# Attention stage: row loads ahead of the weights, five raw tiles for the input weights, query absorption between the token rows

## The chip, the cores and the metric

One core of a Trainium2 chip. The time is that of one execution of the whole program on the device, in microseconds (us); lower is better. The kernel before took 3136.23 us in the median of three runs (3130.83, 3138.18, 3136.23).

## What is computed

Two decoder layers over 1024 tokens of width 1024, in fp32. Layer 0: RWKV-7 time mixing, then a gated feed-forward network (FFN). Layer 1: sparse attention (DSA), then an FFN. Each part ends in a residual and a layer norm. The change lies at the start of the attention, which computes

```python
h = x @ w_in                                   # 1024 x 456: c_q 256 | c_kv 128 | k_idx 64 | w_idx 8
c_q, c_kv = rms_norm(c_q, ...), rms_norm(c_kv, ...); k_idx = layer_norm(k_idx, ...)
q = c_q @ w_uq                                 # 16 heads of 64
q_abs = einsum('bthd,hdc->bthc', q, w_uk)      # logits = q_abs . c_kv * 64**-0.5
```

The kernel forms the product of `w_uq` and `w_uk` once ("absorbs" them; the scale 0.125 is 64**-0.5), so that `q_abs` needs one product per token. Each fp32 matrix product is made of three matmuls on a high and a low part (`mm3`); `split` makes the parts: a cast to the high part on ScalarE, a subtraction for the low part on GpSimd or VectorE.

## The kernel before, in words

The four parts (`rwkv`, `ffn`, `dsa`, `ffn`) are generators, which `drive` interleaves: the start of one is written amid the end of the one before. All instructions are handed to a planner, which fixes each engine's order when the kernel is built: of the instructions whose inputs its own time model holds ready, it takes the one that stands earliest in the program. On the chip every engine, and SP's queue of DMA issues, runs its list strictly in that order.

The end of the first FFN is the product with `w_down` (tile `dn`, lines 65 to 67 by way of `d_mm`). For the second half of the tokens, pairs p = 0 to 8 run over all eight outputs; `d_end` then adds the last two pairs output by output and evicts at L1173: first the four column halves `ch` = 1, after which the attention's first lines are written (L1275 to L1307), then the four halves `ch` = 0 (12 matmuls each). After each of these four, `d_norm` normalizes one 128-row group (L98 to L111 on VectorE, ScalarE and GpSimd) and SP stores it (L149). These are token groups 4 to 7; groups 0 to 3 were stored over 100 us earlier.

The attention's start, in program order: load `uq` and `uk`; the absorption (L1278 to L1295: 64 matmuls into eight banks `wqk`; per bank a scaled copy on ScalarE to `o`, a cast to `hi` on ScalarE, `lo` on GpSimd, two stores to `wqk` in DRAM); eight `w_in` tiles, each loaded into a raw tile `wr` (tag `qr`, two tiles) and split into `win`; the row `grow`. Then come eight steps: `x_load(tt)` loads one token group in two halves (tag `u`, six tiles), and from the third step on `early(2)` takes two entries of a list: `x_T` (eight transposes `pt` and a split into X) and `w_in` (24 matmuls `win` and the norms). Steps 0 to 3 are written before the four last `d_end`, steps 4 to 7 one behind each. After that the hidden rows are transposed (`h_T`, L1368), and the index queries, the indexer, top-k and attention follow.

Where tiles lie matters. Tiles of a pool lie behind one another in the order in which their tags are first used. The attention's pool begins 11 KB (per partition) below the space of the first FFN's pool, and a tile can only be written when the FFN tiles at its addresses are done with. The FFN's pool holds twelve tiles of 4 KB at 11 to 59 KB (tokens `hr`, `hh`, `hl`) and three weight tiles of 16 KB at 59 to 107 KB, which go round by pair. Before, the attention has `u` at 0 to 12 KB, `ph` 12 to 18, `win` 18 to 50, `qr` 50 to 54, `kv` to 58, and three tiles `big` (X and others) to 106.

Of the kernel before, what the change touches and what calls it, by code (L numbers as in the profile page):

```python
# [8 lines left out]
F32R = mybir.dt.float32r  # L9
BF16 = mybir.dt.bfloat16  # L10
AF = mybir.ActivationFunctionType
ALU = mybir.AluOpType
# [33 lines left out]
def f32(ap):  # L46
    return ap.bitcast(F32)


def split(k, raw, hi, lo, hi_eng="a", lo_eng="p"):  # L50

    nc = k.nc
    if hi_eng == "a":
        nc.scalar.copy(hi, raw)  # L54
    elif hi_eng == "v":
        nc.vector.tensor_copy(hi, raw)
    else:
        nc.gpsimd.tensor_scalar(hi, raw, 1.0, 0.0, ALU.mult, ALU.add)
    eng = nc.vector if lo_eng == "v" else nc.gpsimd
    eng.tensor_tensor(lo, raw, f32(hi), ALU.subtract)  # L60
# [1170 lines left out]
def dsa(k, src, dst):  # L1231
    nc, tc = k.nc, k.tc
# [6 lines left out]
    def u(name, dt=F32):  # L1239
        return P_.tile([128, 512], dt, name=name, tag="u", bufs=6)  # L1240

    def tagged(pool, tag, bufs, cols=512):
        return lambda name, dt=F32: pool().tile([128, cols], dt, name=name, tag=tag, bufs=bufs)

    p_, m_ = lambda: P_, lambda: M_
    qr, ph_, qw = tagged(p_, "qr", 2), tagged(p_, "ph", 3), tagged(m_, "qw", 4)
    cm_, ol_ = tagged(m_, "cm", 3, 256), tagged(m_, "ols", 1)

    def w4(name, shape=(128, 1024), dt=F32):
        return P_.tile(list(shape), dt, name=name, tag="tmp", bufs=8)  # L1250

    def ps_tile(tag, name):
        bufs = {"l": 4, "tp": 2, "o": 1, "ol": 1}[tag]
        return (PL if tag == "l" else PS).tile([128, 512], F32, name=name, tag=tag, bufs=bufs)

    def acc(name):
        return ps_tile("l", name)

    def big(name, shape):
        return P_.tile(list(shape), F32R, name=name, tag="big", bufs=3)  # L1260
# [6 lines left out]
    def x_load(tt):  # L1267
        rows[tt] = []
        for g in range(2):
            xr = u("xr")  # L1270
            nc.sync.dma_start(xr, src[tt * 128 : tt * 128 + 128, 512 * g : 512 * g + 512])
            rows[tt].append(xr)


    wqk = k.dram.tile([8, 2, 128, 512], F32, name="wqk")  # L1275
    uq = T_.tile([128, 8, 256], F32, name="uq", tag="toep", bufs=1)
    nc.sync.dma_start(uq, k.w_uq.rearrange("p (h c) -> p h c", h=8))
    for h4 in range(2):  # L1278
        uk = u("uk")
        nc.sync.dma_start(uk, k.w_uk[:, 512 * h4 : 512 * h4 + 512])  # L1280
        for g in range(2):
            gs = slice(64 * g, 64 * g + 64)
            for kt in range(2):
                ps = acc("wqk")
                for h in range(4):
                    hc = slice(128 * h, 128 * h + 128)
                    nc.tensor.matmul(
                        ps[:, hc], uq[gs, 4 * h4 + h, 128 * kt : 128 * kt + 128], uk[gs, hc], start=True, stop=True
                    )
                o, lo = u("wqk"), u("wqkl", F32R)  # L1290
                nc.scalar.activation(o, ps, AF.Copy, scale=0.125)
                hi = ph_("wqkh", F32R)
                split(k, o, hi, lo, "a", CFG["quq"])
                for j, w in enumerate((hi, lo)):
                    nc.sync.dma_start(wqk[4 * g + 2 * h4 + kt, j], f32(w))  # L1295
    win = []
    for kt in range(KT):
        wt = w4("win", (128, 2, 512), F32R)
        raw = qr("wr")
        nc.sync.dma_start(raw[:, :456], k.w_in[kt * 128 : (kt + 1) * 128, :])  # L1300
        split(k, raw[:, :456], wt[:, 0, :456], wt[:, 1, :456], "a", "pv"[kt % 2])
        win.append(wt)
    grow = ph_("grow")
    nc.sync.dma_start(grow, k.dsa_rows[0:1, :].to_broadcast([128, 512]))
    kv = P_.tile([128, 8, 128], F32, name="kv")
    widx = P_.tile([128, 8, 8], F32, name="widx")
    yield  # L1307
# [67 lines left out]
    LAG = CFG['lag']  # L1375
# [7 lines left out]
    def early(n):  # L1383
        for _ in range(n):
            f, tt = pend.pop(0)
            r = f(tt)
            if f is w_in:
                done[0] = r

    for tt in range(8):  # L1390
        x_load(tt)
        if tt >= LAG:
            early(2)
        yield
    M_, PS = pools.add("dsm", first=True, side="left"), pools.psum("dsps", side="left")
    XTh = M_.tile([128, 4, 1024], F32R, name="XTh")
# [18 lines left out]
    for kt in range(2):  # L1415
        raw = qr("wr")
# [481 lines left out]
def trunk(tc, *args):  # L1898
    with ExitStack() as es:
        k = setup(tc, args[:-1], es)  # L1900
        out = args[-1]
        x1, x2, x3 = (Rows(k.dram, f"x{i}") for i in (1, 2, 3))
        drive([rwkv(k, k.x, x1), ffn(k, 0, x1, x2), dsa(k, x2, x3), ffn(k, 1, x3, out)])
# [33 lines left out]
```

## Time and profile before

| | |
|---|---|
| median of three runs | 3136.23 us (3130.83 to 3138.18) |
| profiled execution, its time | 3131.68 us |
| its span, first to last instruction | 3129.9 us |
| TensorE (PE) busy | 2852.7 us, 91% |
| VectorE (DVE), GpSimd (POOL), ScalarE (ACT) busy | 69%, 45%, 43% |
| mean granted TensorE clock | 0.944 of full speed |

The profile is that of one execution. All times below are counted from its first instruction. A line such as L65 is a line of the kernel; helpers such as `mm3` and `split` keep one line for all callers, and the tile names tell them apart. "Idle before" is the time in which the engine stood still just before a group, with what ended it.

### The profile page before, as it was taken

Reading aid. Unit: us, or ns where it says so; the run is one execution under the profiler, and the core shown is the slowest. Engines: PE = TensorE matmul, PEld = TensorE weight load, DVE = VectorE, ACT = ScalarE, POOL = GpSimd, SP = SyncE. Lnnn points to the kernel's source line nnn. Section 1 sums busy time; section 2 is a strip of 40 time slices with the busy share of each in tenths; the row PEclk is TensorE's granted clock in tenths of the full one; section 3 lists DMA queues with packets and bytes.
Section 4 is the critical chain, followed back from the end, with each engine's and each line's share of the span. In section 5 each row is a group of like instructions: output and inputs, shape, how many; then the busy total and the mean of one; then the engine's idle time right before and its main releaser. Section 6 shows DMA issues by size and latency. Waiting matters only on the chain. (4 is left out here: it accounts for less than half of the span.)

```text
span 3129.9 us, 41844 instructions
## 1 busy us (share of the span) xinstructions
PE 2852.7 (91%) x15260; PEld 2249.3 (72%) x15260; DVE 2161.4 (69%) x3609; ACT 1358.0 (43%) x2340; POOL 1406.9 (45%) x947
## 2 busy tenths in 40 slices
PE   7789798899888899999997888889898899999997
PEld 3577666787766777778886766656786677777886
DVE  6777767857676788886142599996575888887142
ACT  4534134232233444444342487785363544444430
POOL 3515115131155677765474122112213667666762
PEclk9889889989899999999999889899999999999999
DMA  6645435435235222235544221113215133333740
GB/s 212 242 146 193 133 106 190 160 106 197 86 120 184 61 81 78 76 90 199 177 168 140 89 86 48 38 34 112 84 46 166 52 81 81 81 94 116 281 168 27
DMA packets 247808, 377.96 MB, mean 121 GB/s; under 512 B 18506, under 2 KB 112074, under 8 KB 247218
## 3 DMA queue, kind: packets, MB, share of 16 engines
q1 hardware_dynamic: 233778, 350.12, 34.3%
q10 hardware_dynamic: 13824, 25.17, 2.2%
q8 instruction: 120, 1.97, 0.3%
q14 instruction: 86, 0.70, 0.1%
HBM read 272.06 MB, written 103.15 MB: 120 GB/s over the span
## 5 line engine op out<-in xcount | busy, mean ns | idle before, releaser
L60 POOL TENSOR_TENSOR wo<-wr,wo 128x512 fp32r<-128x512 f32 x220 | 408.9, 1882 | 290.1 <-ACT wo L54 283.1
L1045 DVE SCALAR_TENSOR_TENSOR cv<-u,vec,cv 128x1023 f32<-128x1023 f32 (+1 forms) x176 | 343.0, 1966 | 58.0 <-ACT cv L1040 56.3
L60 POOL TENSOR_TENSOR wd<-dr,wd 128x1024 fp32r<-128x1024 f32 x88 | 224.8, 2582 | 134.9 <-ACT wd L54 134.9
L67 PE MATMUL dn<-wd,hl 128*128 128x512 f32 x704 | 274.0, 389 | 0.0
L65 PE MATMUL dn<-wd,hh 128*128 128x512 f32 x640 | 249.0, 389 | 0.0
L66 PE MATMUL dn<-wd,hh 128*128 128x512 f32 x640 | 249.0, 389 | 0.0
L65 PE MATMUL p<-xT,wo 128*128 128x512 f32 x528 | 213.3, 404 | 25.7 <-ACT u L1029 19.3
L67 PE MATMUL p<-xT,wo 128*128 128x512 f32 x528 | 208.6, 395 | 5.9 <-POOL wo L60 5.9
L1040 ACT ACTIVATE cv<-u,vec 128x1024 f32<-128x1024 f32 x88 | 109.5, 1245 | 240.2 <-DVE u L1034 240.1
L66 PE MATMUL p<-xT,wo 128*128 128x512 f32 x528 | 208.9, 396 | 3.0 <-DVE xT L60 3.0
L1632 POOL TENSOR_TENSOR cm<-sc,toep 128x256 f32<-128x256 f32 x96 | 75.3, 790 | 296.1 <-DVE mn L1648 227.8
L60 POOL TENSOR_TENSOR wo<-S,wo 128x512 fp32r<-128x512 f32 x88 | 176.3, 2022 | 29.5 <-ACT wo L54 29.5
L60 DVE TENSOR_TENSOR hl<-hr,hh 128x1024 fp32r<-128x1024 f32 x36 | 57.6, 1601 | 160.5 <-ACT hh L54 100.0
L60 POOL TENSOR_TENSOR wl<-wr,wh 128x512 fp32r<-128x512 f32 x56 | 77.6, 1385 | 185.5 <-ACT wh L54 148.7
L67 PEld LDWEIGHTS dn<-wd,hl 128*128 128x128 f32 x704 | 132.2, 188 | 27.5
L65 PEld LDWEIGHTS p<-xT,wo 128*128 128x128 f32 x528 | 100.5, 190 | 63.9 <-ACT u L1029 34.5
L65 PE MATMUL p<-x,wo 128*128 128x512 f32 x352 | 138.5, 394 | 2.9 <-DVE x L60 2.5
L54 ACT CAST wd<-dr 128x1024 fp32r<-128x1024 f32 x88 | 89.3, 1050 | 115.2 <-DMA dr<-in_w_down_dram 51.1
L54 ACT CAST wo<-wr 128x512 fp32r<-128x512 f32 x220 | 126.9, 617 | 26.5 <-POOL wo L60 17.8
L65 PEld LDWEIGHTS dn<-wd,hh 128*128 128x128 f32 x640 | 120.1, 188 | 25.1
L66 PE MATMUL p<-x,wo 128*128 128x512 f32 x352 | 137.9, 392 | 0.0
L66 PEld LDWEIGHTS dn<-wd,hh 128*128 128x128 f32 x640 | 120.1, 188 | 24.7
(403 smaller groups left out, 8130.2 us busy)
## 6 DMA issues: line engine op xcount, KB each, us to landing
wr<-in_w_up_dram SPq DMA_DIRECT2D x88, 512.0 KB, 5.9
dr<-in_w_down_dram SPq DMA_DIRECT2D x88, 512.0 KB, 3.7
hd<-cv SPq DMA_DIRECT2D x44, 512.0 KB, 3.4
hr<-hd SPq DMA_DIRECT2D x44, 512.0 KB, 4.5
wr<-in_w_wo_dram SPq DMA_DIRECT2D x68, 256.0 KB, 3.0
wr<-in_w_rkv_dram SPq DMA_DIRECT2D x48, 256.0 KB, 4.2
kept_w<-wh ACTq DMA_DIRECT2D x48, 256.0 KB, 3.1
kept_w<-wl SPq DMA_DIRECT2D x48, 256.0 KB, 3.1
```

The source lines that it names most:

```text
L54: nc.scalar.copy(hi, raw)
L60: eng.tensor_tensor(lo, raw, f32(hi), ALU.subtract)
L65: mm(ps, lhs[0], rhs[0], start=start, stop=False, **kw)
L66: mm(ps, lhs[0], rhs[1], start=False, stop=False, **kw)
L67: mm(ps, lhs[1], rhs[0], start=False, stop=stop, **kw)
L1040: nc.scalar.activation(o, u, AF.Identity, bias=k.vec[:, cb : cb + 1], scale=k.vec[:, cw[2] : cw[2] + 1])
L1045: nc.vector.scalar_tensor_tensor(o[:, d:], u[:, : 1024 - d], k.vec[:, cw[j] : cw[j] + 1], o[:, d:], ALU.mult, ALU.add)
L1632: (nc.vector if CFG["cm"][h4] == "v" else nc.gpsimd).tensor_tensor(cm[:, :near], mk, toep[g][:, h % 8, 256 - near :], ALU.add)
```

## The change

The loads of token groups 0 and 1 come first. The raw tiles for `w_in` come from two tags, `qr` (two tiles) and `ph` (three). `uq` and `uk` are loaded behind `w_in` and `grow`, `uk` in one DMA into a `big` tile; since `big` is now the first tag used, the pool is laid out as `big` 0 to 48 KB, `u` to 60, `win` to 92, `qr` to 96, `ph` to 102, `kv` to 106. The absorption moves to step 4, thus behind the first of the last four `d_end`. It no longer makes the copy `o`: ScalarE writes `hi` from PSUM with the scale, and VectorE makes `lo` from PSUM; both are `u` tiles. The list of `x_T` and `w_in` is taken at another pace, so that six of its entries instead of four are written ahead of the first of the last four `d_end`.

```diff
+    uk = big("uk", (128, 8, 512))
+
+    def absorb_load():
+        nc.sync.dma_start(uq, k.w_uq.rearrange("p (h c) -> p h c", h=8))
+        nc.sync.dma_start(f32(uk[:, :2]), k.w_uk.rearrange("p (h c) -> p h c", h=2))
+
+    def absorb():            # the same loops and matmuls as before, in a function
...
-                o, lo = u("wqk"), u("wqkl", F32R)
-                nc.scalar.activation(o, ps, AF.Copy, scale=0.125)
-                hi = ph_("wqkh", F32R)
-                split(k, o, hi, lo, "a", CFG["quq"])
+                    hi, lo = u("wqkh", F32R), u("wqkl", F32R)
+                    nc.scalar.activation(hi, ps, AF.Copy, scale=0.125)
+                    nc.vector.scalar_tensor_tensor(lo, ps, 0.125, f32(hi), ALU.mult, ALU.subtract)
...
+    for tt in range(2):
+        x_load(tt)
     win = []
     for kt in range(KT):
         wt = w4("win", (128, 2, 512), F32R)
-        raw = qr("wr")
+        raw = (ph_ if kt % 5 > 1 else qr)("wr")
...
     nc.sync.dma_start(grow, k.dsa_rows[0:1, :].to_broadcast([128, 512]))
+    absorb_load()
...
     for tt in range(8):
-        x_load(tt)
-        if tt >= LAG:
-            early(2)
+        if tt == 4:
+            absorb()
+        if tt >= 2:
+            x_load(tt)
+        early((0, 0, 2, 4, 1, 2, 2, 2)[tt])
         yield
```

## Rows read from the trace of the kernel before

**Rows 1.** Windows of 20 us: busy time and count by engine, clock, DMA.

```profile
1680.00:1700.00 20.00, 18.98 (x117) 16.10 (x116) 10.17 (x27) 12.09 (x24) 12.03 (x11) 1.00 0.53 180
1700.00:1720.00 20.00, 2.70 (x13) 2.15 (x13) 6.40 (x13) 7.95 (x18) 13.16 (x12) 0.66 0.65 230
1720.00:1740.00 20.00, 20.00 (x104) 18.27 (x103) 10.61 (x34) 6.33 (x19) 6.56 (x9) 0.91 0.85 280
```

**Rows 2.** PE's timeline: start, length, operation, count, idle before.

```profile
1682.60 0.39 PE L65 MATMUL dn<-wd,hl 128*128 128x512 f32 x1
1682.92 3.50 PE L1287 MATMUL wqk<-uk,uq 64*128 64x128 f32 x32
...
1695.38 3.47 PE L1287 MATMUL wqk<-uk,uq 64*128 64x128 f32 x32 [1.02 <-DMA uk<-in_w_uk_dram]
...
1700.96 0.39 PE L67 MATMUL dn<-wd,hl 128*128 128x512 f32 x1
1718.64 3.65 PE L1318 MATMUL pt<-ident,xr 128*128 128x128 f32 x16 [17.30 <-DMA xr<-x]
1721.94 0.73 PE L65 MATMUL win<-win,X 128*128 128x456 f32 x1
...
1727.78 1.03 PE L1318 MATMUL pt<-ident,xr 128*128 128x128 f32 x8
1728.58 0.45 PE L65 MATMUL win<-win,X 128*128 128x456 f32 x1
...
1733.64 1.03 PE L1318 MATMUL pt<-ident,xr 128*128 128x128 f32 x8
...
1757.96 0.60 PE L1368 MATMUL ht<-ident,hn 128*128 128x128 f32 x4
```

**Rows 3.** SP's queue of DMA issues, timeline.

```profile
1660.13 24.81 SPq L1300 DMA_DIRECT2D wr<-in_w_in_dram  x8
...
1712.67 0.39 SPq L1304 DMA_DIRECT2D grow<-in_dsa_rows_dram  x1
1713.11 9.52 SPq L1271 DMA_DIRECT2D xr<-x  x10
```

**Rows 4.** What SP's queue waited for, 1640 to 1760 us: total, times, longest.

```profile
SPq L1295 <- POOL wqkl L60: 10.0, 8, 2.8
```

**Rows 5.** ScalarE's and VectorE's timelines: first cast and last split of `win`.

```profile
1671.02 1.05 ACT L54 CAST win<-wr 128x456 fp32r<-128x456 f32 x2 [30.36 <-PE dn L66]
...
1688.03 1.56 DVE L60 TENSOR_TENSOR win<-wr,win 128x456 fp32r<-128x456 f32 x1 [3.44 <-ACT win L54]
```

**Rows 6.** Groups of instructions, 1660 to 1800 us: busy, mean ns, idle before.

```profile
L1291 ACT ACTIVATE wqk<-wqk 128x512 f32<-128x512 f32 x8 | 4.7, 590 | 0.2 <-PE wqk L1287 0.2
L60 POOL TENSOR_TENSOR wqkl<-wqk,wqkh 128x512 fp32r<-128x512 f32 x8 | 11.4, 1445 | 3.8 <-ACT wqkh L54 3.8
L1324 DVE TENSOR_TENSOR X<-pt,X 128x512 fp32r<-128x512 f32 x16 | 10.9, 684 | 5.0 <-ACT X L1323 5.0
L111 DVE TENSOR_TENSOR acc<-acc,lnw 128x512 f32<-128x512 f32 x1 | 0.7, 691 | 1.6 <-POOL acc L110 1.6
L60 POOL TENSOR_TENSOR win<-wr,win 128x456 fp32r<-128x456 f32 x4 | 4.8, 1197 | 30.1 <-ACT win L54 30.1
```

**Rows 7.** Token group 4's norm: its first and last instruction, VectorE's and GpSimd's timelines.

```profile
1689.51 0.67 DVE L1173 SCALAR_TENSOR_TENSOR acc<-acc,dn 128x512 f32<-128x512 f32 x1
...
1696.42 1.60 POOL L111 TENSOR_TENSOR acc<-acc,lnw 128x512 f32<-128x512 f32 x1
```

**Rows 8.** DMA issues, 1555 to 1760 us: count, size, median us to landing.

```profile
x<-acc SPq DMA_DIRECT2D x16, 256.0 KB, 2.2
xr<-x SPq DMA_DIRECT2D x16, 256.0 KB, 4.3
wr<-in_w_in_dram SPq DMA_DIRECT2D x8, 228.0 KB, 2.6
```

**Rows 9.** Windows of 40 us, columns as in the first group: the stage behind.

```profile
1800.00:1840.00 40.00, 31.92 (x138) 24.52 (x139) 37.44 (x145) 30.94 (x82) 11.13 (x18) 0.74 0.19 66
```

More of the change, by code (lines that the diff above doesn't have):

```diff
@@ L1276, in dsa @@
     uq = T_.tile([128, 8, 256], F32, name="uq", tag="toep", bufs=1)
[L1277 to L1289, printed above, removed]
-                o, lo = u("wqk"), u("wqkl", F32R)
-                nc.scalar.activation(o, ps, AF.Copy, scale=0.125)
-                hi = ph_("wqkh", F32R)
-                split(k, o, hi, lo, "a", CFG["quq"])
-                for j, w in enumerate((hi, lo)):
-                    nc.sync.dma_start(wqk[4 * g + 2 * h4 + kt, j], f32(w))
+    uk = big("uk", (128, 8, 512))
[3 more added lines that the diff above has]
+    def absorb():
+        for h4 in range(2):
+            for g in range(2):
+                gs = slice(64 * g, 64 * g + 64)
+                for kt in range(2):
+                    ps = acc("wqk")
+                    for h in range(4):
+                        hc = slice(128 * h, 128 * h + 128)
+                        nc.tensor.matmul(
+                            ps[:, hc], uq[gs, 4 * h4 + h, 128 * kt : 128 * kt + 128], f32(uk[gs, h4, hc]),
+                            start=True, stop=True,
+                        )
+                    hi, lo = u("wqkh", F32R), u("wqkl", F32R)
+                    nc.scalar.activation(hi, ps, AF.Copy, scale=0.125)
+                    nc.vector.scalar_tensor_tensor(lo, ps, 0.125, f32(hi), ALU.mult, ALU.subtract)
+                    for j, w in enumerate((hi, lo)):
+                        nc.sync.dma_start(wqk[4 * g + 2 * h4 + kt, j], f32(w))
+    for tt in range(2):
+        x_load(tt)
     win = []
```

## Prediction

> **What bounds the kernel now.** I read the profile from coarse to fine: busy shares, windows, PE's timeline around the change, then SP's queue, which says why PE stood. PE is busy for 2852.7 us of 3129.9, so what can be won is where PE stands. In the windows the reader is to see one hole: from 1700 to 1720 PE works 2.70 of 20 us, at a clock of 0.66, between windows that are nearly full [rows 1]. PE's timeline places it: the last `dn` matmul starts at 1700.96, the next instruction is the transpose of the first token rows at 1718.64, after 17.30 us idle, ended by the DMA of these rows [rows 2]. The rows of groups 0 to 3 had long been stored. Their loads were issued only at 1713.11 because they stand in SP's list behind `grow` and the sixteen stores of `wqk` [rows 3], and eight of those waited, 10.0 us in all, for the low parts on POOL [rows 4], which POOL made between norm steps at 1445 ns each [rows 6]. So the chain was: absorption, POOL, stores, row loads, transposes. The change breaks it.
>
> **What goes.** Three terms on PE's path. First the hole, 17.30 us. Second, 1.02 us in which the second half of the absorption waited for `uk` [rows 2]; it is now one DMA, issued well before its use. [...] The phase from 1718.64 to 1757.96, eight `x_T` and six `w_in`, took 39.3 us. At the upper level one `x_T` takes 0.80 (1727.78 to 1728.58) and one `w_in` 5.06 (1728.58 to 1733.64) [rows 2], so 8 x 0.80 + 6 x 5.06 = 36.8; the hole cost 2.5 more. Sum of the three: 20.8 us. No matmul is removed, so this is the ceiling.
>
> **What the weights cost.** The raw tiles move to 92 to 102 KB, all under the FFN's third weight tile (91 to 107 KB). Pairs go round three tiles, and that one serves pair 8, whose matmuls end at 1671.02; this is what the first cast waited for before, too [rows 5]. Before, two raw loads left at 1660.13, when pair 7 was done [rows 3]; now none before 1671. The price: the first cast comes 2.6 us (a landing, [rows 8]) later. The return: five loads go out together instead of two. Load six waits for the first raw tile's split: 1671 + 2.6 + cast 0.6 + low part on POOL 1.2 [rows 6] = 1675.4; it lands at 1678, and the last of the three, with a cast and a split, is done near 1682 (1681 to 1685, as several loads share the engines). Before it was 1689.6 [rows 5]. PE needs the weights at the first `w_in`, near 1684.6 (below). So this costs between nothing and 1 us, and I take nothing: the `dn` matmuls still left cover it. The first four row halves lie at 48 to 56 KB, over tokens of pairs 6 and 7: loaded by about 1665.
>
> **The absorption.** The eight scaled copies, 0.590 us each, go from ACT: 4.7 us. The low parts go from POOL (11.4 us) to VectorE, reading PSUM [rows 6]. This instruction, a scale and a subtraction on PSUM and SBUF, isn't in the trace; the nearest are `X`'s low part from PSUM, 0.684 us, and the eviction L1173 from PSUM, 0.67 [rows 6, 7]; POOL's 1.445 is the far end. I take 0.68: 5.5 us more on VectorE, which was busy 27.2 of the 60 us to 1740 [rows 1]. Hidden by PE's matmuls; without that cover it is paid in the norms that wait behind it, at most 8 x 0.68. A subtraction costs the same from PSUM (0.684) as from SBUF (0.691) [rows 6]. [...]
>
> **What is given back.** The new limit is token groups 4 to 7. Before, their norms ran inside the hole; now `x_T` of these groups is reached while they run. From the eviction of a group to its rows in SBUF: norm 1689.51 to 1698.02, 8.5 us [rows 7]; store 2.2, load 4.3 [rows 8]; 15.0 in all. Now PE in strict program order, from 1682.6. The four `d_end` need 18.75 (1682.60 to 1701.35) - 6.97 (absorption) - 1.02 = 10.8, so 2.7 each [rows 2]. Two `x_T` 1.6; the split of X about 1.3 (0.6 and 0.68); `w_in`, `x_T`, `w_in`, `x_T` 11.7: 1697.2. First `d_end` to 1699.9, absorption to 1706.9, `w_in` to 1711.9, second `d_end` to 1714.6. Group 4 is there at 1699.9 + 15 = 1714.9: no stall. `x_T`, `w_in`, third `d_end`: 1723.5. Group 5 comes at 1714.6 + 15 = 1729.6: 6 us stall. `x_T`, `w_in`, fourth `d_end`: 1738.2; group 6 on time; `x_T`, `w_in` to 1744.3; group 7 at 1753.2: 9 us stall. The hidden rows' transposes then start at 1754.0 instead of 1757.96: a gain of 4.0. That is one end. The other: the planner knows such delays and pulls the next `w_in` and `d_end` ahead of an `x_T` that isn't ready, and the transposes of finished rows ahead of the last one. Then the third `d_end` ends at 1720.6, the fourth at 1728.4, PE hardly stands, and the transposes start by 1738: a gain of 19 to 20. [...] I take the middle of 4.0 and 20: 12 us.
>
> **Queues passed.** On SP the first rows, then `w_in`, `grow`, `uq` and `uk` stand ahead of the stores; nothing that was needed sooner is behind them, as `uq` and `uk` are wanted only near 1700. The sixteen stores of `wqk` (read again only after the index queries) now stand among the loads of groups 4 to 7 and the norms' stores. Behind the hidden rows' transposes the order of work is as before, and VectorE, busy 37.44 of 40 us from 1800 on [rows 9], is fed by them; I carry the gain to the end unchanged.
>
> **The sum.** 3131.7 (profiled execution: span 3129.9 and 1.8 around it) - 12 = 3119.7. The median of the runs shown is 4.5 above that execution, and 3136.2 - 12 = 3124.2. As any of these runs could be the one measured, I forecast 3122.
>
> **Rivals.**
> (1) Strict order: PE's list keeps the program's order, groups 5 and 7 are late. For it: nothing but the planner's clock moves them. Against: it skips what it holds unready. Gain 4.0: 3127.7 by the profiled execution, no change that can be measured.
> (2) Slower: the `u` tiles. The absorption sends sixteen tiles through six that the row loads also use, and a tile is free only when its store has landed. Per bank: matmuls 0.87, cast 0.6, low part 0.68, issue 0.35, landing 2.2 (the nearest store): 4.7 us, three banks at a time, so 1.6 us a bank and 12.5 us for eight instead of 7.0. Where `x_load(4)` gets its tiles only behind the last store, group 4 comes about 4 us late as well, and in strict order the transposes start at 1754 + 5.5 + 4 = 1763.5: 5.5 us later than before, 3137.2 (3142 by the median). It decides if SP issues group 4's load after the last `wqk` store. Against it: before, three banks were also in flight, and PE ran each half at full pace [rows 2].
> (3) Given back behind: top-k and the indexer, VectorE's stage, absorb the shift because their own order changes with the planner's clock: about 3132. Against it: all they read comes out of the transposes.
>
> **How the numbers follow.** Two runs of this kernel tell about 0.2% apart, 6.3 us. Forecast with its own range, gains of 7 to 20.8: chance 0.70, 3111 to 3129. Strict order 0.13 (no change), given back 0.07 (no change), slower 0.10. So faster 0.71, same 0.18, slower 0.11, a hundredth moved each way for the spread of the runs. The range runs from the ceiling by the profiled execution, 3131.7 - 20.8 = 3111, to a gain of 3 by the median, 3133; it leaves out the slower rival and half of the third.
>
> **What would show it.** Right: no PE gap above 5 us between 1690 and 1740; the first `xr` loads issued before 1661, the first transposes near 1682; `win` complete before 1686; `wqkl` on VectorE at about 0.68 us; the hidden rows' transposes between 1738 and 1751; later windows shifted by the same amount. The gap before each `x_T` of groups 5 to 7 is the given-back part. Wrong: a gap of 15 us or more before one of these, or SP holding a row load behind `wqk` stores; or the transposes early and the end not.

## The result, and the profile after

The changed kernel takes 3114.61 us in the median of four runs (3112.03 to 3117.03); the kernel before, run beside it, 3137.07 us (3130.83 to 3138.18). The ratio is 0.9935, 95% interval 0.9913 to 0.9956. On a second chip with more runs (the last experiment) it was 3119.70 against 3132.15 us, ratio 0.9950 (0.9932 to 0.9968). So it is faster, by some 10 to 27 us; forecast were 3122 us and a gain of 12.

Medians that wander by several microseconds don't say how much of this is the change, so I cut each profiled execution in four at events that every kernel here has: the first `hd` store of the first FFN, the first `ch` = 1 eviction behind it, the first transpose of hidden rows, and the end. The first cut is the first start in the row of line L1055, here of the kernel before and then of the changed kernel (columns: minimum, median and maximum ns of one, first and last start in us):

```profile
L1055 SPq DMA_DIRECT2D hd<-cv x44: 319/339/339, 1066.6 to 2892.5; - x44
```

```profile
L1055 SPq DMA_DIRECT2D hd<-cv x44: 319/338/339, 1063.8 to 2875.5; - x44
```

The next two cuts are the ends of a window; first the kernel before, then the changed kernel, columns as in [rows 1]:

```profile
1673.96:1757.96 84.00, 65.69 (x357) 57.88 (x356) 40.44 (x120) 34.11 (x85) 36.16 (x36) 0.90 0.54 183
```

```profile
1671.21:1740.50 69.29, 65.67 (x357) 56.81 (x355) 39.84 (x128) 30.86 (x80) 23.07 (x24) 0.98 0.57 192
```

| part, us | before | after | difference |
|---|---|---|---|
| head, to the first `hd` store (RWKV, code unchanged) | 1066.65 | 1063.75 | -2.9 |
| FFN, to the first `ch` = 1 eviction | 607.31 | 607.46 | +0.15 |
| the stretch that is changed, to the first `ht` | 84.00 | 69.29 | -14.7 |
| tail, to the end (span 3129.9 and 3113.0) | 1371.9 | 1372.5 | +0.6 |

The FFN part is 607.3 to 607.5 us in all fourteen executions profiled, so the third row is sharp. All the gain that belongs to the change, 14.7 us, is in the changed stretch. The 2.9 us of the head are not the change's: its code is the same, and the changed kernel itself had a head of 1073.3 us in its second profile. Of the stretch, PE stood for 84.00 - 65.69 = 18.3 us before and 3.6 us after. The same three windows as in [rows 1], of the changed kernel, show the hole gone and a small one left:

```profile
1680.00:1700.00 20.00, 19.82 (x129) 17.85 (x127) 11.84 (x40) 8.11 (x22) 1.72 (x2) 1.00 0.25 85
1700.00:1720.00 20.00, 19.62 (x107) 16.45 (x106) 12.95 (x37) 10.64 (x26) 6.50 (x7) 1.00 0.83 300
1720.00:1740.00 20.00, 16.94 (x83) 14.74 (x82) 10.62 (x43) 7.27 (x21) 9.31 (x11) 0.91 0.55 168
```

PE's timeline of the changed kernel, which answers to [rows 2]:

```profile
1680.08 1.91 PE L1326 MATMUL pt<-ident,xr 128*128 128x128 f32 x16
...
1695.50 3.50 PE L1291 MATMUL wqk<-uk,uq 64*128 64x128 f32 x32
...
1716.10 0.63 PE L1326 MATMUL pt<-ident,xr 128*128 128x128 f32 x4 [0.38 <-DVE lnm L98]
...
1726.12 1.29 PE L1326 MATMUL pt<-ident,xr 128*128 128x128 f32 x8 [3.03 <-DMA xr<-x]
...
1727.98 0.58 PE L65 MATMUL win<-win,X 128*128 128x456 f32 x1
1728.36 0.58 PE L66 MATMUL win<-win,X 128*128 128x456 f32 x1
...
1740.50 0.60 PE L1376 MATMUL ht<-ident,hn 128*128 128x128 f32 x4
```

The transposes of the first rows now start before the absorption and wait for nothing. One wait is left, 3.03 us ahead of group 5's transposes (1726.12), and the matmuls from 1727.98 on start 0.38 us apart instead of 0.21: the granted clock from 1727.65 to 1731.27 is 0.53. SP's list of the changed kernel, which answers to [rows 3], shows what feeds them:

```profile
1646.72 12.15 SPq L1271 DMA_DIRECT2D xr<-x  x4
1668.48 4.66 SPq L1307 DMA_DIRECT2D wr<-in_w_in_dram  x6
...
1711.44 0.60 SPq L1299 DMA_DIRECT2D wqk<-wqkl  x1
1712.14 1.32 SPq L1271 DMA_DIRECT2D xr<-x  x2
...
1722.68 0.88 SPq L1271 DMA_DIRECT2D xr<-x  x2
```

Groups 0 and 1 are loaded before the raw weights; group 4's load (1712.14) still stands right behind the last store of `wqk`. The new split, and ScalarE's part of it, from the groups of the changed kernel (columns as in [rows 6]):

```profile
L1297 DVE SCALAR_TENSOR_TENSOR wqkl<-wqk,wqkh 128x512 fp32r<-128x512 f32 x8 | 5.5, 684 | 4.5 <-ACT wqkh L1296 3.3 <-DMA wqk<-wqkl 1.2
L1296 ACT ACTIVATE wqkh<-wqk 128x512 fp32r<-128x512 f32 x8 | 4.7, 598 | 5.4 <-DMA wqk<-wqkh 5.2 <-PE wqk L1291 0.2
```

### The profile page after: what moved, and what is told of

The parts are those of the page before. It is cut to its first block, busy times and chain, and to the rows that moved or that the text cites. A ratio compares the mean times of both kernels' runs of the same rounds, so it can differ in the third digit from the quotient of the medians.

```text
span 3113.0 us, 41835 instructions
## 1 busy us (share of the span) xinstructions
PE 2847.3 (91%) x15260; PEld 2241.3 (72%) x15260; DVE 2167.5 (70%) x3617; ACT 1355.6 (44%) x2332; POOL 1397.3 (45%) x939
## 5 line engine op out<-in xcount | busy, mean ns | idle before, releaser
L65 PE MATMUL p<-x,wo 128*128 128x512 f32 x352 | 139.3, 396 | 1.3 <-DVE x L60 0.8
L66 PE MATMUL p<-x,wo 128*128 128x512 f32 x352 | 138.9, 395 | 0.0
L67 PE MATMUL p<-x,wo 128*128 128x512 f32 x352 | 138.6, 394 | 0.0
L66 PEld LDWEIGHTS dn<-wd,hh 128*128 128x128 f32 x640 | 120.1, 188 | 25.1
```

Of the source, the lines that this page charges most:

```text
L65: mm(ps, lhs[0], rhs[0], start=start, stop=False, **kw)
L66: mm(ps, lhs[0], rhs[1], start=False, stop=False, **kw)
L67: mm(ps, lhs[1], rhs[0], start=False, stop=stop, **kw)
```

## The experiments

Each kernel is the changed one, or the one before, with one edit. "The stretch" is the third row of the table above. The expectations of 1 to 8 count it from the first `hd` store, thus 607.4 us more; the table gives both. The 95% intervals of the ratios reach about 0.002 to either side, so that the whole times hardly tell these kernels apart. What follows rests on the stretch, in one profile of each kernel; the changed kernel and kernel 1 have two, which agree to 0.3 us. What of the stretch is not PE's idle time is its busy time, and this differs too, as the same 356 or 357 matmuls take longer where the granted clock is lower: 63.5 to 65.2 us at a clock of 1.00, 65.7 to 71.9 below it.

| kernel | stretch, us | from the `hd` store | PE idle in the stretch | clock in the stretch | time against before, ratio |
|---|---|---|---|---|---|
| before | 84.0 | 691.3 | 18.3 | 0.90 | |
| changed | 69.3; again 69.3 | 676.8; 676.7 | 3.6 | 0.98 | 0.9935; again 0.9950 |
| 1 absorption at the front | 66.9; again 66.7 | 674.3; 674.1 | 3.2 | 1.00 | 0.9950; again 0.9926 |
| 2 before, split from PSUM | 75.1 | 682.5 | 8.0 | 0.93 | 0.9972 |
| 3 no chain of norms | 64.3 | 671.6 | 0.5 | 1.00 | 0.9958 |
| 4 absorption later, other pace | 80.7 | 688.1 | 10.7 | 0.89 | 0.9998 |
| 5 as 1, split on GpSimd | 74.9 | 682.2 | 7.1 | 0.93 | 0.9960 |
| 6 as 2, `uk` in one DMA | 74.3 | 681.7 | 5.1 | 0.93 | 0.9977 |
| 7 two raw tiles | 70.1 | 677.6 | 5.0 | 1.00 | 0.9954 |
| 8 as 1, group 0 ahead | 76.8 | 684.2 | 4.9 | 0.91 | 0.9962 |
| 9 split on GpSimd | 73.4 | 680.8 | 6.0 | 0.95 | 0.9962 |
| 10 old pace | 69.2 | 676.7 | 4.0 | 1.00 | 0.9958 |

**1. Is it the move of the absorption that closes the hole?** The absorption goes back to the front.

```diff
+    absorb_load()
+    absorb()
     for tt in range(2):
         x_load(tt)
...
-    absorb_load()
...
-        if tt == 4:
-            absorb()
```

> The changed kernel with the absorption back at the front: its loads, matmuls, splits and stores stand ahead of the token rows again; the split from PSUM, the five raw tiles and the list's pace stay. Measured on the stretch from the first store of the first FFN's hidden rows (hd) to the first transpose of the attention's hidden rows (ht): 691.4 us before, 676.7 after. Theory (the hole was the slow store chain absorption, POOL, stores, row loads; whichever breaks it closes the hole): with the split from PSUM three banks in flight take 1.6 us each, the stores end near 1694, the rows land near 1700 when the dn matmuls end at 1697: a gap of 3 to 6 us before the first pt and 2 us of clock, but no wait for groups 5 to 7, since all dn matmuls are early; stretch 676 to 680. Rival (the move of the absorption itself closes the hole): a gap of over 10 us stays before the first pt, stretch 685 or more.

Measured: 66.9 us, shorter than the changed kernel and 1.7 us below the theory's range. SP's list and PE's timeline of this kernel:

```profile
1697.71 0.32 SPq L1299 DMA_DIRECT2D wqk<-wqkl  x1
1698.12 2.22 SPq L1271 DMA_DIRECT2D xr<-x  x4
```

```profile
1686.15 6.62 PE L1291 MATMUL wqk<-uk,uq 64*128 64x128 f32 x64
1702.59 0.60 PE L1327 MATMUL pt<-ident,xr 128*128 128x128 f32 x4
```

The rows stand behind the sixteen stores as before the change, but the last of these leaves 11.6 us after PE began the absorption (1697.71 - 1686.15), where it took some 30 us before (1682.92 to 1712.67, [rows 2, 3]). PE has `dn` matmuls until then: no idle stands in front of 1702.59. The move isn't needed to close the hole, and here it costs 2.4 us.

**2. The split from PSUM alone**, on the kernel before.

```diff
-                o, lo = u("wqk"), u("wqkl", F32R)
-                nc.scalar.activation(o, ps, AF.Copy, scale=0.125)
-                hi = ph_("wqkh", F32R)
-                split(k, o, hi, lo, "a", CFG["quq"])
+                hi, lo = u("wqkh", F32R), u("wqkl", F32R)
+                nc.scalar.activation(hi, ps, AF.Copy, scale=0.125)
+                nc.vector.scalar_tensor_tensor(lo, ps, 0.125, f32(hi), ALU.mult, ALU.subtract)
```

> The kernel before with one edit: hi on ScalarE and lo on VectorE straight from PSUM; order, loads, raw tiles and pace as before. Theory (the stores waited for POOL): the last low part is done near 1700 instead of 1712, the row loads follow, the gap before the first pt shrinks from 17.3 to 4 to 9 us; stretch hd to ht 679 to 684. Rival (SP's order and the late uk hold the rows, not POOL): gap still 14 us or more, stretch 688 or more.

Measured: 75.1 us, within the theory, and 8.9 of the 14.7. PE's timeline and SP's list:

```profile
1711.17 3.98 PE L1317 MATMUL pt<-ident,xr 128*128 128x128 f32 x16 [6.87 <-DMA xr<-x]
```

```profile
1694.61 0.33 SPq L1280 DMA_DIRECT2D uk<-in_w_uk_dram  x1
...
1707.24 0.32 SPq L1294 DMA_DIRECT2D wqk<-wqkl  x1
```

The wait of 17.30 us is 6.87. By SP's list, what is left has the same form: the second half of `uk` is loaded at 1694.61, behind the first half's stores, the last store leaves at 1707.24, and the rows behind it. The edit does two things: it takes the low part from GpSimd to VectorE and leaves out ScalarE's copy (0.590 us each); they were not tried apart. [rows 4] puts 10.0 us of SP's waits down to GpSimd's low parts.

**5. The other way round**: kernel 1 with the split as it was (the edit of 2 backwards).

> e1_absorb_front with the split of the kernel before (copy and cast on ScalarE, low part on GpSimd): the absorption at the front, uk in one DMA, five raw tiles, new pace. Theory (the split's engine sets the end of the stores): eight low parts at 1.3 to 1.45 us on GpSimd, with win's four between them, end 3 to 6 us later than in e1, the rows too; e1's dn matmuls still cover most; stretch hd to ht 676 to 681 against 674.3 in e1. Rival 1 (GpSimd's split is the whole cause): the gap of over 10 us is back, stretch 685 or more. Rival 2 (the late uk was the cause, the split is nothing): 674 to 675.

Measured: 74.9 us, between the two theories. SP's list, then PE's and VectorE's timelines:

```profile
1706.12 0.32 SPq L1300 DMA_DIRECT2D wqk<-wqkl  x1
1706.49 1.89 SPq L1271 DMA_DIRECT2D xr<-x  x4
```

```profile
1717.41 0.75 PE L65 MATMUL win<-win,X 128*128 128x456 f32 x1 [3.99 <-DVE X L1334]
```

```profile
1715.93 0.16 DVE L104 SCALAR_TENSOR_TENSOR lnnm<-lnm,lnrs 128x1 f32<-128x1 f32 x1 [1.35 <-POOL lnrs L103]
```

The split on GpSimd costs 8.0 us at the front, 3.8 in idle time and 4.1 in busy time. The rows stand behind the stores again, but PE waited only 1.6 us for them, in four pieces. The longest wait, 3.99 us, is for VectorE's split of X, which stood on VectorE's list behind norm steps that in turn waited for GpSimd (1.42 and 1.35 us); GpSimd had had the eight low parts until 1706.1. What the norms lost by that was not separated. Behind the wait of 3.99 us the `win` matmuls started 0.38 us apart and more up to 1726.21, and 0.21 from 1726.52 on.

**9. The split on GpSimd amid the rows**, the changed kernel with the edit of 2 backwards.

> The changed kernel with the split of the query weights as it was before: copy to SBUF on ScalarE, hi half on ScalarE, lo half on GpSimd at 1.445 us each. From the first eviction of the first norm group to the first ht transpose the changed kernel takes 69.3 us, the kernel before 84.0. Theory (once the absorption stands amid the rows, eight GpSimd splits keep the group-4 load behind the query-weight stores for longer, as they kept all the row loads before): stores end 5 to 8 us later, the group-4 load with them, and the stretch takes 73 to 77 us. Rival (amid the rows nothing urgent stands behind the stores, so the engine of the split is of no account there): 69 to 71 us.

Measured: 73.4 us: the theory's range, at its lower end. SP's list and PE's timeline:

```profile
1724.16 0.32 SPq L1300 DMA_DIRECT2D wqk<-wqkl  x1
1724.58 0.87 SPq L1271 DMA_DIRECT2D xr<-x  x2
```

```profile
1712.87 1.16 PE L1291 MATMUL wqk<-uk,uq 64*128 64x128 f32 x8 [1.93 <-ACT wqk L1296]
...
1728.84 0.63 PE L1327 MATMUL pt<-ident,xr 128*128 128x128 f32 x4 [0.50 <-DMA xr<-x]
```

Group 4's load leaves at 1724.58, 45.9 us after the first eviction (1678.68), against 40.9 in the changed kernel (1712.14 - 1671.21), as the theory has it. But PE waited only 0.50 us for these rows. What it has more of is two waits for ScalarE's copy out of a bank (0.69 and 1.93 us) and 1.8 us of busy time, at a clock of 0.95. So with the move the split is worth 4.1 us instead of 8.0. That the first rows no longer stand behind the stores fits this, but was not shown to be the reason.

**6. One DMA for `uk`**, into a `big` tile, on kernel 2.

```diff
+    uk = big("uk", (128, 8, 512))
+    nc.sync.dma_start(f32(uk[:, :2]), k.w_uk.rearrange("p (h c) -> p h c", h=2))
     for h4 in range(2):
-        uk = u("uk")
-        nc.sync.dma_start(uk, k.w_uk[:, 512 * h4 : 512 * h4 + 512])
...
```

> e2_direct_only with one more edit: uk in one DMA into a big tile (which also moves the pool's tiles as in the changed kernel); two raw tiles, old pace, absorption at the front. Theory (in e2 the second half of the absorption still waits for uk, whose load stands behind the first half's stores): all 64 matmuls run at once near 1683, the stores end 4 to 8 us earlier, the gap before the first pt falls from 6.9 us to under 3, stretch 674 to 678 against 682.5. Rival (e1's gain over e2 came from the raw tiles and the pace): stretch 681 to 683.

Measured: 74.3 us, in the rival's range. SP's list, then VectorE's and PE's timelines:

```profile
1693.16 10.11 SPq L1299 DMA_DIRECT2D wr<-in_w_in_dram  x6
...
1718.28 0.32 SPq L1294 DMA_DIRECT2D wqk<-wqkl  x1
```

```profile
1702.28 0.63 DVE L60 TENSOR_TENSOR win<-wr,win 128x456 fp32r<-128x456 f32 x1 [3.52 <-ACT win L54]
```

```profile
1703.56 3.97 PE L1287 MATMUL wqk<-uk,uq 64*128 64x128 f32 x24 [1.21 <-DVE wqkl L1292]
```

A tile in `big` changes the layout, since `big` is then the first tag used. The two raw tiles fall under the FFN's last weight tile, and six loads that wait for them (until 1703.27) now stand ahead of the stores. On ScalarE and VectorE the splits of these weights stand ahead of those of the absorption: VectorE waits 3.52 us for ScalarE's cast, and PE 1.21 us for the first low parts. Behind this wait 24 matmuls of the absorption take 3.97 us, where the 32 ahead of it took 3.50, and those of `dn` start 0.43 us apart (1710.78 to 1714.62), then 0.23. The waits for rows did shrink, from 6.87 to 1.6 us in two pieces, as the theory had it; PE's busy time is 2.0 us more than in kernel 2. What the one DMA wins, the late raw tiles take. Kernel 1, which differs from this one by the three more raw tiles, the place of the rows' and weights' loads and the pace, takes 66.9.

**7. Two raw tiles instead of five**, the changed kernel with `raw = qr("wr")`.

> The changed kernel with two raw tiles for w_in again. Theory (the weights are then late for the first w_in, as the raw tiles are free only near 1668 and the eight loads go two by two): win is complete 4 to 6 us later than 1681, PE waits 2 to 5 us amid or before the first w_in, or runs dn there; stretch 678 to 682 against 676.8. Rival (dn matmuls cover it, as the prediction took): 676 to 677.

Measured: 70.1 us, 0.8 more, between the two ranges. PE's timeline:

```profile
1687.17 0.48 PE L65 MATMUL win<-win,X 128*128 128x456 f32 x1 [0.43 <-ACT win L54]
1688.40 0.47 PE L66 MATMUL win<-win,X 128*128 128x456 f32 x1 [0.75 <-POOL win L60]
...
1728.65 1.28 PE L1326 MATMUL pt<-ident,xr 128*128 128x128 f32 x8 [3.26 <-DMA xr<-x]
```

Amid the rows nothing urgent stands behind the raw loads, and PE waits 1.2 us for the weights. Group 5's rows are waited for as in the changed kernel (3.26 us), but here the `win` matmuls behind the wait start 0.21 us apart, and the granted clock of the stretch is 1.00.

**3. What is the rest?** In the changed kernel groups 4 to 7 read the rows of groups 0 to 3, which have long been stored; the norms and their stores stay.

```diff
-            nc.sync.dma_start(xr, src[tt * 128 : tt * 128 + 128, 512 * g : 512 * g + 512])
+            r_ = tt % 4 * 128
+            nc.sync.dma_start(xr, src[r_ : r_ + 128, 512 * g : 512 * g + 512])
```

> The changed kernel, but token groups 4 to 7 are read from the rows of groups 0 to 3, which are long stored: the attention's input is wrong there, and its x_T of these groups no longer waits for the norms. Theory (what was given back is the wait for groups 5 to 7 and the clock after it): the 3.0 us wait and the 10 slow matmuls go, stretch 670.5 to 673 against 676.7. Rival (the row loads are held in SP's queue or by tiles u, not by the norms): the wait stays, stretch 675 to 677.

Measured: 64.3 us, within the theory (671.6 from the `hd` store). The window of this kernel:

```profile
1677.99:1742.26 64.27, 63.79 (x356) 55.59 (x355) 39.39 (x121) 31.06 (x79) 19.71 (x20) 1.00 0.56 190
```

PE stands 0.5 us and the granted clock is 1.00. So the chain from eviction over norm, store and load to the transposes costs the changed kernel 69.29 - 64.27 = 5.0 us: 3.1 standing and 1.9 in PE's busy time, of which the slow matmuls behind the wait are 1.5 (ten of them in 3.62 us, where ten at 0.21 take 2.1).

**4. Can the order hide that chain?** The absorption goes one step further back, and the list is taken later.

```diff
-        if tt == 4:
+        if tt == 5:
             absorb()
...
-        early((0, 0, 2, 4, 1, 2, 2, 2)[tt])
+        early((0, 0, 2, 2, 1, 2, 3, 3)[tt])
```

> The changed kernel with the absorption one step later (behind the second of the last four d_end) and the list taken as 0, 0, 2, 2, 1, 2, 3, 3: all dn matmuls end before the first x_T of groups 4 to 7, with the absorption and w_in between. Theory (only the norms' chain of 15 us is left): no wait above 1 us before any x_T, stretch 671 to 674, total 3 to 5 us below the changed kernel. Rival (the chain is then bound by VectorE, where low parts, norms and splits meet): the same waits elsewhere, stretch 676 to 679.

Measured: 80.7 us, worse than both theories. PE's, VectorE's and SP's timelines:

```profile
1721.53 1.13 PE L1291 MATMUL wqk<-uk,uq 64*128 64x128 f32 x8 [1.71 <-DVE wqkl L1297]
...
1727.78 1.09 PE L1326 MATMUL pt<-ident,xr 128*128 128x128 f32 x4 [5.13 <-issue]
```

```profile
1726.39 0.69 DVE L111 TENSOR_TENSOR acc<-acc,lnw 128x512 f32<-128x512 f32 x1 [1.62 <-POOL acc L110]
1727.00 0.68 DVE L1297 SCALAR_TENSOR_TENSOR wqkl<-wqk,wqkh 128x512 fp32r<-128x512 f32 x1
```

```profile
1734.77 5.09 SPq L1271 DMA_DIRECT2D xr<-x  x6
```

Put among the norms, the absorption goes as slowly as these. All of PE's idle time in the stretch lies ahead of 1730: five waits that the profile puts down to VectorE (5.5 us in all, the longest 1.71) and one of 5.13 us for which it names no releaser. This one ends 0.1 us behind a split on VectorE (1727.00 + 0.68), which stood on VectorE's list behind norm steps that waited 1.54 and 1.62 us for GpSimd; that PE waited for this split is likely and not shown. So it is the rival's mechanism, VectorE where low parts, norms and splits meet, at more than its price. The clock of the window is 0.89, and PE's busy time is 4.4 us more than in the changed kernel. The loads of three groups leave late as well, behind the last store (1734.77), but from 1733.60 to the end of the stretch PE has no idle time: these rows held nothing.

**10. The old pace** of the list, (0, 0, 2, 2, 2, 2, 2, 2).

> The changed kernel with the pace of the early work as it was (2 pieces rather than 4 at group 3, 2 rather than 1 at group 4). Theory (the pace only decides which rows wait, the chain eviction, norm, load, transpose of groups 4 and 5 is the same length): 69 to 71.5 us from the first eviction to the first ht transpose, against 69.3. Rival (the four pieces at group 3 are what fills TensorE while group 4's rows are on their way): 72 to 75 us, with a wait of 3 us or more ahead of group 4's transposes.

Measured: 69.2 us, idle 4.0: just within the theory's lower end. With the absorption amid the rows the new pace wins nothing.

**8. Group 0's load ahead of the absorption**, on kernel 1, in the hope of a version better than both.

```diff
     absorb_load()
+    x_load(0)
     absorb()
-    for tt in range(2):
-        x_load(tt)
+    x_load(1)
```

> e1_absorb_front, but token group 0 is loaded ahead of the absorption and group 1 behind it. Theory (what is left in e1 is the start after the dn matmuls: first transposes, split of X, with no matmuls to cover them): the first transposes run amid the dn matmuls, stretch 671 to 673.5 against 674.3. Rival (the absorption with four u tiles instead of six is slower and its stores later, groups 1 to 3 come late): stretch 675 to 680.

Measured: 76.8 us, 684.2 from the `hd` store: the rival's way, and 4.2 us beyond its range. SP's list, PE's timeline, and waits of this kernel from two stretches (total, times, longest us):

```profile
1680.68 0.33 SPq L1299 DMA_DIRECT2D wqk<-wqkh  x1
...
1700.39 0.32 SPq L1299 DMA_DIRECT2D wqk<-wqkl  x1
1700.81 1.36 SPq L1271 DMA_DIRECT2D xr<-x  x3
```

```profile
1677.03 3.50 PE L1291 MATMUL wqk<-uk,uq 64*128 64x128 f32 x32
1681.48 3.78 PE L1291 MATMUL wqk<-uk,uq 64*128 64x128 f32 x16 [0.95 <-DVE wqkl L1297]
```

```profile
SPq L1436 <- PE wqk L1291: 5.3, 1, 5.3
...
ACT wqkh L1296 <- DMA wqk<-wqkh: 2.9, 2, 1.7
DVE wqkl L1297 <- DMA wqk<-wqkl: 2.3, 2, 1.6
```

The sixteen stores leave over 19.7 us instead of 9.8 (1687.96 to 1697.71 in kernel 1), and the rows of groups 1 to 3 behind them. The copies and splits wait 5.2 us for `u` tiles whose stores have not landed, of which group 0 now holds two, and a load of `toep`, which the planner put among the stores, holds SP for 5.3 us until PE has done the absorption's last matmuls, since `uq` lies in that tile. But late rows are not what PE paid for: it waited 0.92 us for rows, as in kernel 1 (0.91). Of the 9.9 us over kernel 1 only 1.6 are idle time; 8.3 are busy time (71.93 to 63.68). Behind the wait of 0.95 us for a split, sixteen matmuls of the absorption take 3.78 us where 32 took 3.50, and for 13.6 us without a pause (1681.48 to 1695.08) `dn` matmuls that follow one another start 0.43 to 0.60 us apart, later 0.23.

**11 and 12. The changed kernel and kernel 1 again**, beside each other.

> The changed kernel unaltered, on the chip of the next run. Both theories: 69.3 us from the first eviction to the first ht transpose, as in its first profile; the stretch from the first hd store to that eviction 607.4 us; the time of the whole within 3 us of 3114.6, with the head up to the first hd store making up whatever the difference is.

> The changed kernel with the query weights absorbed ahead of the rows, a second time and beside the changed kernel itself. Theory (with the direct split and five raw tiles the place of the absorption is worth about 2 us, and the front is the better place): 66.9 us from the first eviction to the first ht transpose, as in its first run, and a whole that is 1 to 4 us shorter than the changed kernel's beside it. Rival (the first run's 2.4 us was by chance): 68.5 to 70 us and no difference in the whole.

Measured: the changed kernel 69.3 us, head 1073.3, median 3119.70, which is 5.1 us from the first batch where 3 were expected; kernel 1, in its window,

```profile
1673.85:1740.54 66.69, 63.49 (x357) 55.44 (x356) 42.86 (x128) 31.04 (x79) 27.11 (x29) 1.00 0.70 233
```

66.7 us, head 1066.4, median 3111.88, ratio 0.9926 (0.9900 to 0.9952). In the two profiles of the changed kernel the head makes up 9.5 of the 10.1 us between the spans. In the stretch kernel 1 is shorter than the changed kernel by 2.4 and 2.6 us in two pairs. The whole shows it 7.8 us shorter here, more than the 1 to 4 expected, and in the first batch not (0.9950 to the changed kernel's 0.9935 on another chip), and the intervals overlap: that it is the better kernel is shown for the stretch alone.

## Why the prediction was right, step by step

The time fell where it was forecast, and for the reason given: SP's list held the first rows behind stores that waited for GpSimd. By the forecast's own steps:

- **The hole and the wait for `uk`** (17.30 + 1.02): PE idle of the stretch fell from 18.3 to 3.6 us. These 14.7 are the whole gain.
- **The clock term** (2.5) brought nothing in sum. Before, it lies in the first two `x_T` and the first `w_in` behind the hole, 9.14 us for 6.66 by the forecast's 0.80 and 5.06, at a granted clock of 0.73 (1718.64 to 1727.78); the 5.86 us from which the 0.80 and 5.06 were taken (1727.78 to 1733.64) have 1.00. PE's busy time in the stretch is 65.69 us before and 65.67 after: ten matmuls at a granted clock of 0.53 behind the 3.03 us wait give back 1.5 of it, and where the other 1.0 went was not singled out. The forecast had no term for slower matmuls behind a wait that is left.
- **The weights** (nothing, `win` done near 1682): the first raw loads left at 1668.48, as forecast right behind pair 8's last matmul (1668.06, the 1671 of before less the shorter head), and the last split ended at 1680.61. Nothing waited for them.
- **The split on VectorE** (0.68 each): 0.684, and ScalarE's cast 0.598. The operation from PSUM takes no longer than the 0.691 of one from SBUF [rows 6].
- **What is given back** (8.8) was the term of the sum that was mis-sized: 20.8 - 14.7 = 6.1. Of it 5.0 is the chain of norms (experiment 3); what the other 1.1 is was not singled out. In PE's terms the 6.1 are 3.6 us of idle time and the 2.5 of the clock term. The chain itself was right: group 5, from its eviction at 1711.56 to its transposes at 1726.12, took 14.6 us for 15.0. The planner did pull `w_in` and `d_end` ahead, so one wait of 3.03 and one of 0.38 us stand where strict order had 6 and 9. The middle between the two ends was a guess, and it was 2.7 us too cautious.
- **Strict order** (rival 1) is ruled out by these two waits; **given back behind** (rival 3) by the tail, 1371.9 and 1372.5 us (1369.7 to 1374.7 in all fourteen profiles), which would otherwise be longer by what the stretch gained.
- **The `u` tiles** (rival 2): its condition came true and its price did not. Group 4's load did leave right behind the last store (1712.14), 3.0 us later than the store of its norm (issued at 1706.90, 2.2 to land, [rows 8]) would have let it; the forecast had named this as a sign of being wrong. PE had `w_in` and `d_end` to do, and stood 0.38 us ahead of that group's transposes, which the profile puts down to VectorE. The stores are slower still in 9, 4 and 8, and PE's waits for rows are no longer there than here; what costs time are waits for banks and splits, and the lower clock (0.95, 0.89 and 0.91 in the stretch, for 0.98).
- **The median**: forecast 3122, measured 3114.61 and then 3119.70. By the profiled execution it was 3119.7 against 3114.82: 2.7 us are the stretch and 2.9 the head, which has nothing to do with the change; the FFN and the tail take 0.7 back.

What I did not see ahead is which edit earns the time. I priced the change as one chain that it breaks by the move. The runs show two ways to break it: the faster split alone wins 8.9 of the 14.7 us (2), and with `uk` in one DMA, five raw tiles and the loads' new places 17.1 (1), with the absorption still ahead of the rows. The move without the faster split, but with the other edits, wins 10.6 (9); the move alone was not run. Behind the move the split is worth 4.1 us instead of 8.0; raw tiles (0.8) and pace (0) were tried by themselves only there. Beside kernel 1 the move costs 2.4 us, 2.0 of them PE's busy time (65.67 to 63.68) with its 1.5 at the granted clock of 0.53. That this comes of the norms of groups 4 to 7, amid which the absorption now runs, is an argument and was not shown.

## What to carry to other kernels

A queue that issues DMAs in order can be part of the critical path, as SP's was here (PE stood 17.30 us): when an engine stands for a load whose data is old, look at what stands ahead of that load in the list, and who makes those wait. Then there are two remedies, to move the load or to make what stands ahead quick; try each alone, since together they can pay less than their sum (here 8.9 and 10.6 us, and 14.7 with both). Late loads by themselves prove nothing: in experiments 4, 8 and 9 they left late too, and what PE waited for was mostly something else. Look at what ends PE's waits, and at its busy time as well as its idle time. And cut the profile at events that all versions share: here a stretch of 70 us repeated to 0.3 us, while whole times of one kernel spread over 10 us and more.

## What the runs showed that was not expected

- The same code in front of the changed part took 1056.9 to 1082.5 us in the fourteen profiled executions (the first `hd` store), the changed kernel alone 1063.8 and 1073.3, while the FFN behind it took 607.3 to 607.5 in each. Where it was read, the granted clock is lower in the longer head: 0.90 in the changed kernel (1063.75 us, PE busy for 936.1) and 0.89 in the kernel before (1066.65, 937.6). From the start to 1000 us, as the mean of ten windows, it is 0.90 in experiment 10, which has the shortest head, and 0.88 in 6, which has the longest; PE is busy there for 881.8 us with 6285 matmuls and for 882.5 with 6208. In the FFN the clock is 1.00 both before and in the changed kernel. What makes the clock of the head differ from one execution to the next stays open.
- What comes behind a wait can cost more than the wait, and its length does not tell how much. In the changed kernel the wait of 3.03 us is followed by 3.6 us at a granted clock of 0.53; without it (experiment 3) the stretch is 5.0 us shorter, with 1.9 us less in PE's busy time. In experiment 7 a wait of 3.26 us at the same place is followed by matmuls 0.21 us apart, and in experiment 8 one of 0.95 us by 13.6 us in which `dn` matmuls start 0.43 us apart and more, instead of 0.23. What decides between them stays open.
